# Layer 0's recurrence projections of a two-layer decoder trunk: three 256-column matmuls per weight block, or a 512- and a 256-column matmul and a fold

## The chip, the core and the metric

The kernel runs on one core of one Trainium2 chip. The metric is the device time of one execution in microseconds (us). The kernel before took 2241.95 us as the median of 3 runs (2240.21 to 2243.34).

The core has five engines with a queue each. PE (TensorE) multiplies a moving tile by a stationary block of 128x128 weights and adds the result up in a bank of PSUM, the memory behind it; the profile shows the load of the stationary block as PEld. DVE (VectorE) and ACT (ScalarE) do elementwise work and are the ones that read PSUM here. POOL and SP issue transfers. Every engine runs its instructions in the order in which the program was built, and waits at an instruction whose operands are not ready.

## The reference, cut to what matters

A sequence of 256 tokens of width 2048 goes through two layers and a final norm. Layer 0 mixes tokens by two recurrences:

```python
proj = h @ w_in                                   # 2048 x 6144
x_lru, y_lru, q_h, f_h, v_h, g_h = split(proj)    # six groups of 1024 columns
lru = rg_lru(causal_depthwise_conv(x_lru), ...)   # two gates, then a scan over tokens
lru = lru * gelu(y_lru)
hg = hgrn2(q_h, f_h, v_h, g_h, ...)               # 8 heads of 128, chunkwise
mix = concatenate([lru, hg]) @ w_out
```

Layer 1 is an attention layer; both layers end in a squared-ReLU MLP of width 8192. All data are float32, and the kernel keeps nearly that precision: each operand is split into a high part (rounded to the type that PE takes) and a low part (the rest), and a product is high x high + high x low + low x high.

## The kernel before, in words

**Units of weights.** Weights come in units of 128x2048 floats (1 MB), in a fixed list, by transfers that SP issues. `Weights.split` (L94 to L98) turns each half of a unit into `hi` (an ACT copy, L97) and `lo` (a DVE subtraction, L98). Three raw units, five `hi` halves and five `lo` halves are held at a time.

**A projection** (`project`, L305) multiplies one unit, 16 blocks of 128x128, by the 16 blocks of the activations `bufa`. Each activation block is 128x512: 256 columns of high part, then 256 columns of low part (one column a token). The result is one 128-column slice of the projection for all 256 tokens, added up in one bank `p` of PSUM; the pool `pmm` has three banks. Two ways of doing it stand in the kernel:

- `cross` (L163): for each block, the high weights against all 512 columns, which puts high x high in the bank's first half and high x low in the second; then, in a second pass over the 16 blocks, the low weights against the 256 high columns, into the second half as well. The two halves must be added when the bank is read. The MLP's first matrix and layer 1's q and k use it.
- `direct` (L169): for each block three matmuls of 256 columns, all into the first half. Nothing is left to add.

**Reading a bank in layer 0.** `scaled` (L360) writes the projection times the norm's factor `rs` to SBUF. For `direct` it is one DVE operation (L363). Otherwise ACT copies the second half to `t1` (L366), DVE adds the first half (L367) and DVE multiplies by `rs` (L368). Both ways stand under `urgent`, which the build's list scheduler ranks highest.

**The stage around the change** is layer 0's recurrence. Its steps stand in the list ORDER: `v0 h0 x0 h1 x1 h2 x2 h3 x3 v1 h4 x4 ... h7 x7 g0 y0 y1 y2 y3 g1 y4 y5 y6 y7`.

- `h` (`hgrn`, 8 heads): three projections (q, f, g), and between them a chain of levels: PE makes a 128x64 product `pl` twice (L423), DVE or ACT puts it in the score tile `st` (L426, L431, L433, L419), DVE multiplies `qk` by decay factors (L440), and the next level needs that. After eight levels come `po` (L447 to L449), a norm over a head (L453 to L458, with a chain of tiny DVE operations, L273 to L278), two transposes `pt` (L461), a multiplication by the gate (L467) and the split of the result into its block of `bufb` (L189 on ACT, L190 on DVE).
- `x` (`lru_in`, 8): one projection and a convolution (L477, L479).
- `g` (`lru_gates`, 2): eight small products of two blocks, which always use `direct`, then sigmoid, tanh, exp and sqrt on ACT (L158), each kind with a table load, and on DVE L497 to L506 with a scan over tokens.
- `y` (`lru_out`, 8): one projection, GeLU (ACT L513 and L158, DVE L514 to L517), and the split into `bufb`.
- `v` (2) makes values with `tokens` (512-column matmuls); it is not touched.

After the stage `w_out` follows: for each 512 columns of output, four units over the blocks of `bufb`, heads 0 to 3 first, then heads 4 to 7, then the two LRU groups.

`mm` (L145) chains all these matmuls in program order, so PE can't do a later projection first; the other products (`pl`, `po`, `pt`) are fitted in between by the scheduler, which lists instructions by an estimate of when each can run.

Of the kernel before, what the change touches and what calls it, by code (L numbers as in the profile page):

```python
# [40 lines left out]
def trunk_kernel(ctx, tc, x, xtok, cols, tab, masks, pos, fin, w_in, w_gate, w_out, w_qkv, w_o, w1, w2, out):  # L41
# [132 lines left out]
            mm(p, h, mov[:, S:], start=False, stop=False)  # L174
            mm(p, l, mov[:, :S], start=False, stop=last)

    HA, XA, YA = direct, direct, direct

    def folded(p, name="z", bufs=None):
        with urgent():  # L180
# [635 lines left out]
```

## Time and profile before

| | |
|---|---|
| time of the profiled execution | 2240.74 us |
| its span | 2239.0 us |
| granted TensorE clock over the span | 0.998 |
| layer 0's recurrence, about 21 to 336 us of the span | 32 projections and the first gates up to 280 us, then y0 to y3, the second gates and y4 to y7 |
| waits of PE from 21 to 431 us | 1.3 us at L447, 1.6 us for `bufa` and `lo` |

The profiled execution's time is 1.7 us more than its span. Times on the page are of this one execution. A row of a timeline or of a group gives an instruction's recorded duration; instructions of one engine overlap at their ends, so a queue's pace is read from the distance between starts. Idle time of an engine is put down to what ended it.

### The profile page before, as it was taken

Reading aid. Unit: us, or ns where it says so; the run is one execution under the profiler, and the core shown is the slowest. Engines: PE = TensorE matmul, PEld = TensorE weight load, DVE = VectorE, ACT = ScalarE, POOL = GpSimd, SP = SyncE. Lnnn points to the kernel's source line nnn. Section 1 sums busy time; section 2 is a strip of 40 time slices with the busy share of each in tenths; the row PEclk is TensorE's granted clock in tenths of the full one; section 3 lists DMA queues with packets and bytes.
Section 4 is the critical chain, followed back from the end, with each engine's and each line's share of the span. In section 5 each row is a group of like instructions: output and inputs, shape, how many; then the busy total and the mean of one; then the engine's idle time right before and its main releaser. Section 6 shows DMA issues by size and latency. Waiting matters only on the chain.

```text
span 2239.0 us, 30359 instructions
## 1 busy us (share of the span) xinstructions
PE 2218.6 (99%) x12196; PEld 1934.2 (86%) x12196; DVE 1409.1 (63%) x2212; ACT 1073.6 (48%) x1537; POOL 1.9 (0%) x7
## 2 busy tenths in 40 slices
PE   9999999999999999999999999999999999999997
PEld 8999998888888888888888888888888888888886
DVE  7777886565565565465567878556655645655654
ACT  6444585554444344344454445455434434434443
POOL 0000000000000000000000000000000000000000
PEclk9999999999999999999999999999999999999999
DMA  8444445455555555555554454555555555555553
GB/s 308 151 155 166 151 156 202 172 190 192 198 188 188 190 193 189 199 188 188 188 188 170 169 172 170 196 180 186 188 189 197 191 194 188 188 189 200 190 192 113
DMA packets 58717, 414.51 MB, mean 185 GB/s; under 512 B 6528, under 2 KB 7296, under 8 KB 9168
## 3 DMA queue, kind: packets, MB, share of 16 engines
q1 hardware_dynamic: 58320, 412.20, 52.4%
q8 instruction: 95, 1.56, 0.3%
q0 software_dynamic: 256, 0.38, 0.1%
q14 instruction: 46, 0.38, 0.1%
HBM read 410.70 MB, written 2.10 MB: 184 GB/s over the span
## 4 chain that ended last, share of the span: by engine, by line
PE 97%; ACT 1%; DVE 0%; issue 0%; DMA 0%; SPq 0%; ACTq 0%; DVEq 0%
PE p L146 94%; PE pl L423 1%; PE pl L548 0%; ACT hi L97 0%; PE pl L646 0%; DMA xall<-in_x 0%; PE po L667 0%; PE pd L659 0%; ACT L158 0%; DVE bufa L193 0%; PE pd L407 0%; PE pl L645 0%; ACT gi L158 0%; ACT bufa L192 0%; PE po L668 0%
## 5 line engine op out<-in xcount | busy, mean ns | idle before, releaser
L98 DVE TENSOR_TENSOR lo<-raw,hi 128x1024 fp32r<-128x1024 f32 (+1 forms) x774 | 932.1, 1220 | 603.1 <-ACT hi L97 431.8
L97 ACT CAST hi<-raw 128x1024 fp32r<-128x1024 f32 (+1 forms) x774 | 811.1, 1049 | 879.8 <-PE p L146 808.7
L146 PE MATMUL p<-bufa,hi 128*128 128x512 f32 (+1 forms) x3840 | 858.8, 357 | 3.1 <-DVE bufa L193 3.1
L146 PE MATMUL p<-hi,bufb 128*128 128x512 f32 x2560 | 793.9, 390 | 0.0
L146 PEld LDWEIGHTS p<-bufa,hi 128*128 128x128 f32 x3840 | 671.8, 189 | 95.4 <-DVE bufa L193 4.2
L146 PEld LDWEIGHTS p<-hi,bufb 128*128 128x128 f32 x2560 | 480.0, 188 | 98.7
L146 PE MATMUL p<-bufa,lo 128*128 128x256 f32 x3200 | 519.8, 284 | 0.0
L146 PE MATMUL p<-lo,bufb 128*128 128x512 f32 x1280 | 498.4, 389 | 0.0
L146 PEld LDWEIGHTS p<-bufa,lo 128*128 128x128 f32 x3200 | 451.5, 191 | 12.1
L146 PEld LDWEIGHTS p<-lo,bufb 128*128 128x128 f32 x1280 | 240.4, 188 | 49.4
L190 DVE TENSOR_TENSOR bufb<-z,bufb 128x256 fp32r<-128x256 f32 x136 | 57.7, 424 | 127.7 <-ACT bufb L189 127.7
L146 PE MATMUL p<-hi,bufa 128*128 128x512 f32 x384 | 122.6, 396 | 1.1 <-ACT hi L97 1.1
L182 ACT COPY t<-p 128x256 f32<-128x256 f32 x128 | 47.6, 372 | 111.7 <-PE p L146 111.7
L146 PEld LDWEIGHTS p<-hi,bufa 128*128 128x128 f32 x384 | 72.0, 188 | 16.5 <-ACT hi L97 2.0
L146 PE MATMUL p<-lo,bufa 128*128 128x512 f32 x192 | 76.3, 397 | 1.8 <-DVE lo L98 1.8
L189 ACT CAST bufb<-z 128x256 fp32r<-128x256 f32 x136 | 54.5, 401 | 17.2 <-DVE z L571 14.4
L536 DVE SCALAR_TENSOR_TENSOR xall<-p,nm,xall 128x512 f32<-128x512 f32 x64 | 47.8, 748 | 20.1 <-PE p L146 20.1
L571 DVE SCALAR_TENSOR_TENSOR z<-z 128x256 f32<-128x256 f32 x128 | 54.4, 425 | 4.4
L184 DVE TENSOR_TENSOR z<-p,t 128x256 f32<-128x256 f32 x128 | 53.3, 417 | 0.0
L247 ACT ACTIVATE z<-xall 128x512 bf16<-128x512 f32 x32 | 20.2, 631 | 54.5 <-DVE xall L536 54.5
L146 PEld LDWEIGHTS p<-lo,bufa 128*128 128x128 f32 x192 | 36.1, 188 | 10.5 <-DVE lo L98 3.7
L423 PE MATMUL pl<-qk 128*128 128x64 f32 x224 | 31.1, 261 | 0.0
(197 smaller groups left out, 729.1 us busy)
## 6 DMA issues: line engine op xcount, KB each, us to landing
raw<-in_w SPq DMA_DIRECT2D x256, 1024.0 KB, 4.8
raw<-in_w_qkv SPq DMA_DIRECT2D x48, 1024.0 KB, 4.8
raw<-in_w_in SPq DMA_DIRECT2D x46, 1024.0 KB, 4.8
raw<-in_w_out SPq DMA_DIRECT2D x16, 1024.0 KB, 4.8
raw<-in_w_o SPq DMA_DIRECT2D x16, 1024.0 KB, 4.8
xall<-in_xtok SPq DMA_DIRECT2D x1, 2048.0 KB, 9.3
raw<-in_w_gate SPq DMA_DIRECT2D x2, 1024.0 KB, 4.8
out<-xall SPq DMA_DIRECT2D x4, 512.0 KB, 4.0
```

The costliest lines, as they stand in the source:

```text
L97: A.copy(h, w)
L98: V.tensor_tensor(l, w, h.bitcast(F32), OP.subtract)
L146: chain[:] = [after(T.matmul(*args, **kw), chain)]
L182: A.copy(t, p[:, S:])
L184: V.tensor_tensor(z, p[:, :S], t, OP.add)
L189: A.copy(dst[:, :S], src)
L190: V.tensor_tensor(dst[:, S:], src, dst[:, :S].bitcast(F32), OP.subtract)
L247: A.activation(q, xres[:, j, n * 512:n * 512 + 512], AF.Square, accum_out=self.ss[:, j, n:n + 1])
L423: T.matmul(pl[:, j], kq[:, js], halves(qp[:, js], c, True), start=True, stop=True)
L536: V.scalar_tensor_tensor(xres[:, j, at], ps[j], 1.0 if scale is None else scale[:, j:j + 1], xres[:, j, at], op0=OP.mult, op1=OP.add)
L571: V.scalar_tensor_tensor(z, z, 0.0, z, op0=OP.max, op1=OP.mult)
```

## The change

The three names that choose how layer 0's projections are done go from `direct` to `cross`: `HA` (the 24 projections of the heads), `XA` (8, `lru_in`) and `YA` (8, `lru_out`).

```diff
-    HA, XA, YA = direct, direct, direct
+    HA, XA, YA = cross, cross, cross
```

Each of these 40 projections has 16 blocks, so 640 x 3 matmuls of 256 columns become 640 of 512 columns and 640 of 256, and the loads of stationary blocks go from 1920 to 1280. Through `scaled`, which asks `if acc is direct`, each bank is now read by L366 on ACT and by L367 and L368 on DVE in place of L363 on DVE. The gates keep `direct`. The units, the transfers and the list ORDER stay as they are; SP's and POOL's instructions keep their order. PE's, DVE's and ACT's order is made anew by the scheduler.

## The prediction

> **What bounds the kernel now.** I read the shares of busy time first, then the chain that ended last, then the timeline of PE in two stages, and last DVE's load by stretch and the waits.
>
> From the page, engine shares and the chain:
>
> ```profile
> PE 2218.6 (99%) x12196; PEld 1934.2 (86%) x12196; DVE 1409.1 (63%) x2212; ACT 1073.6 (48%) x1537; POOL 1.9 (0%) x7
> ...
> PE 97%; ACT 1%; DVE 0%; issue 0%; DMA 0%; SPq 0%; ACTq 0%; DVEq 0%
> ```
>
> PE sets the end nearly everywhere, so a change of PE's pace counts in full wherever DVE and ACT keep up. What matters is the pace (distance of starts), not the duration. PE's timeline, first in the recurrence (direct: hi, hi, lo), then in the MLP, where cross already runs:
>
> ```profile
> 281.11 0.40 PE L146 MATMUL p<-bufa,hi 128*128 128x256 f32 x2
> 281.35 0.28 PE L146 MATMUL p<-bufa,lo 128*128 128x256 f32 x1
> 281.47 0.40 PE L146 MATMUL p<-bufa,hi 128*128 128x256 f32 x2
> ```
>
> ```profile
> 501.06 3.82 PE L146 MATMUL p<-bufa,hi 128*128 128x512 f32 x16
> 504.71 2.08 PE L146 MATMUL p<-bufa,lo 128*128 128x256 f32 x16
> 506.63 3.82 PE L146 MATMUL p<-bufa,hi 128*128 128x512 f32 x16
> ```
>
> A block of direct takes 0.36 us (281.11 to 281.47; 0.1198 us a matmul over longer stretches), a projection 16 x 3 x 0.1198 = 5.75 us. Under cross, 16 matmuls of 512 columns take 3.65 us (0.228 each) and 16 of 256 take 1.92 us (0.120): 5.57 us.
>
> DVE's load decides the rest. Busy time by stretch, columns PE, PEld, DVE, ACT:
>
> ```profile
> 190.00:200.00 10.00, 10.00 (x87) 10.00 (x86) 8.30 (x17) 4.27 (x6) 0.00 (x0) 1.00 0.57 202
> ...
> 280.00:290.00 10.00, 10.00 (x86) 10.00 (x85) 7.21 (x14) 9.94 (x17) 0.00 (x0) 1.00 0.44 129
> 290.00:300.00 10.00, 8.71 (x74) 8.50 (x73) 9.34 (x20) 7.88 (x16) 0.00 (x0) 1.00 0.48 185
> 300.00:310.00 10.00, 10.00 (x86) 10.00 (x85) 10.00 (x30) 6.93 (x17) 0.52 (x1) 1.00 0.54 190
> ```
>
> Up to 270 us DVE is 69 to 89% busy. From the first gates (PE starts them at 273.17) to 340 us DVE or ACT is full. PE's one wait there is 1.3 us:
>
> ```profile
> 295.04 0.49 PE L447 MATMUL po<-vg,st 128*128 128x128 f32 x2 [1.29 <-ACT st L433]
> ```
>
> **The change, part by part.**
>
> *Matmuls.* 40 projections x (5.75 - 5.57) = **-7.2 us**, all on PE's path. The Trainium skill, "TensorE: Matmul & The Clock Gate", section "Back-to-back issue gap", has a matmul of N columns at N / 2.4 GHz + 2.5 ns: one saved fixed cost of 2.5 ns a block, an estimate of 1.6 us for 640 blocks, by which the sum below would be 5.6 us higher. The trace does not agree (0.228 against 2 x 0.1198, 11.5 ns a block), and the measurement decides.
>
> *The fold.* In place of L363 (0.335 us from start to start) come L366 on ACT (0.31) and L367 and L368 on DVE (0.335 each): 40 x 0.335 = 13.4 us more on DVE, 12.4 on ACT. Before the first gates DVE's idle share hides this: adding up DVE's queue of the changed order with the paces of the trace gives 37.0 us of work beside 47.4 of PE from h0's f to the second f, and 40.5 beside 49.8 in the last heads. A bank is released later by the copy's 0.3 us and DVE's queue; with three banks there are two projections, 11.1 us, of slack. Cost here: 0 if hidden; each us that DVE is late past that is 1 us. I take 1 us, near the 0 that the busy first half of DVE shows today; the upper end is 8 us, one us a head (the L447 wait of 1.3 us once a head).
>
> *What moves.* Because the folds rank as urgent, the scheduler lets the heads' level chains slide behind. In the order before, head 7 is at its third level when the first gates begin, and its transposes stand inside y5. In the changed order head 6 begins its first level there, and head 7's transposes stand in the second unit of w_out, two matmuls ahead of the block that needs their result. So ten levels and one and a half heads' norms come into the stretch in which DVE is full already. SP's and POOL's queues are as before, and nothing waits for a transfer.
>
> *That stretch, worked out.* Time 0 is PE's start of the first gates; paces as read from the trace (weight split on DVE 1.14, 256-column DVE operation 0.335, scan 0.60, predicated copy or tiny operation 0.20, ACT `hi` copy 0.94, ACT 256-column function 0.36, square root or copy 0.31, table load 1.28).
>
> 1. PE to the end of y1: 8 gate products x 0.72 + 2 x 5.57 + 5 level pairs x 0.366 + 6 small products x 0.12 = 19.5.
> 2. ACT then, in its new order: copy of y1, one sigmoid, 4 tanh, table, exp, `hi`, 3 exp, table, 2 sqrt, 2 small copies, third sqrt = 0.31 + 0.36 + 1.44 + 1.28 + 0.36 + 0.94 + 1.08 + 1.28 + 0.62 + 0.40 + 0.31 = 8.4. DVE's L504 waits for that sqrt: 27.9.
> 3. DVE from there to L467 of head 7: 15 weight splits 17.1, 8 scans 4.8, 70 operations of 256 columns 23.5, 40 short ones of 0.20 (5 level copies, 20 tiny norm steps, 4 of L500, 11 for the rotary tables, which are queued ahead too) 8.0, 4 of 0.12 0.5: 53.9. The same adding-up for the order before, from the first L497 to the last y's L517, gives 61.6 and with the 7.5 us of DVE idle that the waits show 69.1, beside some 70 on the trace; so I add 1.8%: 54.8. L467 starts at 82.7.
> 4. L467, ACT's split and DVE's split, 0.42 + 0.40 + 0.42: PE goes on at **84.0**.
>
> PE's own work to that matmul: 16 gate products 11.5, 8 projections 44.6, 35 w_out matmuls x 0.228 = 8.0, 14 level pairs 5.1, 18 small ones 2.2 = 71.4. PE is late by **12.6 us**: by my reading some 4 at the second gates (y2 and y3 still hold two of three banks), some 2 at w_out's second bank, the rest ahead of head 7's block. The 1.3 us at L447 goes: that wait's st copy is done by 31.0 and PE gets there at 31.2.
>
> Bounds: if ACT never delays DVE, L467 is bound by DVE's sum alone, 0.8 + 75.2 = 76.0 and PE at 77.2, 5.9 late; with as much DVE idle again as before's whole stretch (7.5), it is 16 to 20.
>
> *Sum.* -7.2 - 1.3 + 12.6 + 1 = **+5 us** on the profiled execution's 2240.74 (span 2239.0 and 1.7 around it), 2246; the median of the runs shown is 1.2 above that execution, so I forecast **2247 us**.
>
> **Rivals.**
>
> *A, the folds stay hidden (ends on the other side).* If DVE's real idle time in the tail is used up by the new order, so that L467 of head 7 starts within 4 us of PE's arrival, the sum is -7.2 - 1.3 + 1 + 0 to 4: 2234.5 to 2238. For: PE was never held by DVE's sum before, and the MLP runs cross at full pace. Against: DVE at 10.00 of 10 in 300 to 310, and step 3. It decides below a delay of 4 us. Chance 0.17; between it and the forecast (delay 4 to 8 us, 2238 to 2242) 0.1.
>
> *B, DVE late in the heads too.* Every level is a round of PE, DVE and PE, and a fold that sits ahead of L440 holds PE at the next L423. At 1 us a head, 8 us on top: 2250 to 2259. For: the slid levels show that DVE's time was short in the planned order; against: 81% load by step 2's sums. Chance 0.18.
>
> *C, the clock falls during the stall.* After the last matmul (2226.9) the granted clock is 1.00 to 2230, 0.80 in the next us and then 0.50, so it falls after 3.9 us without matmuls. Head 7's wait may be one gap of 6 us. Nothing in the trace shows the way back; between nothing and as long as the fall took at half pace it costs 0 to 2 us: 2247 to 2249. Inside the forecast; chance 0.3 of it. The Trainium skill, same page, section "What's actually happening", has the way back after a busy window of about 3.4 us, an estimate of 1.7 us.
>
> **How the numbers follow.** Forecast with C 0.55 (2242 to 2250, by the delay's bounds of 8 to 16), A 0.17, between 0.1, B 0.18. Leaving out half of A and a quarter of B gives the range 2236 to 2257. A measurement of this kernel tells about 0.2%, 4.5 us, from no change. Below 2237.5: 0.16; above 2246.4: B and the upper 6 in 10 of the forecast, 0.51; between: 0.33.
>
> **What would show it.** Right: 128x512 and 128x256 matmuls of the recurrence at 0.228 and 0.120 from start to start; no PE waits to speak of before the first gates; then some 12 us of PE idle from the first gates to w_out's second unit, put down to DVE or ACT, the longest ahead of head 7's block, right behind L461; DVE near 10 of 10 there. Wrong: the same pace but no such idle (A), or idle at L423 throughout (B), or matmuls of 512 columns slower than 0.228 beside DVE's and ACT's reads.

## The result, and the profile after

The changed kernel takes 2249.16 us (median of 7 executions, 2248.22 to 2251.92) against 2241.78 us for the kernel before (7 executions, 2240.21 to 2243.34). The ratio is 1.0034, with a 95% interval of 1.0024 to 1.0044: slower by 7.4 us. The forecast was 2247. The profiled execution took 2251.92 us (span 2250.2), 2.8 more than the median, and it is compared below with the profiled execution before, 2240.74 us: 11.2 us more.

Engine shares and the chain, from the page of the changed kernel:

```profile
PE 2220.6 (99%) x11556; PEld 1906.6 (85%) x11556; DVE 1417.7 (63%) x2252; ACT 1089.4 (48%) x1577; POOL 1.9 (0%) x7
...
PE 97%; DVE 1%; ACT 1%; DMA 0%; issue 0%; SPq 0%; ACTq 0%; DVEq 0%; POOLq 0%
```

PE has 640 instructions fewer, which by the pace alone should have taken some 7 us off, and is still busy 2.0 us longer, so some of its work became slower. DVE has 40 operations more, ACT 40. The chain's shares say little of this: DVE has gone from 0% to 1%.

PE's timeline in the heads (start, duration, line, names, moving tile, count):

```profile
226.51 2.07 PE L146 MATMUL p<-bufa,lo 128*128 128x256 f32 x16
228.42 0.86 PE L146 MATMUL p<-bufa,hi 128*128 128x512 f32 x3
...
236.21 3.82 PE L146 MATMUL p<-bufa,hi 128*128 128x512 f32 x16
239.87 0.28 PE L146 MATMUL p<-bufa,lo 128*128 128x256 f32 x1
```

Start to start, 16 matmuls of 256 columns take 1.91 us (0.119 each) and 16 of 512 take 3.66 (0.229): the new projections run at the pace of the MLP's.

The milestones show where the time went. The first gates' first matmul, in the kernel before and then in the changed one:

```profile
273.17 0.40 PE L146 MATMUL p<-bufb,hi 128*128 128x256 f32 x2
261.30 0.40 PE L146 MATMUL p<-bufb,hi 128*128 128x256 f32 x2
```

It starts **11.9 us earlier**: 32 x 0.18 = 5.8 are pace, and most of the rest is head work that now stands behind it (9 of 56 level pairs at 0.366 are 3.3, the ends of two heads, L418, L447 to L449 and L461, 1.1). The first MLP matmul starts at 435.43 in place of 425.76, **9.7 us later**. So the stretch between the two has grown by 21.5 us. PE's waits from 21 to 440 us, by what ended them (total, times, longest):

```profile
PE pt L461 <- ACT ho L458: 5.7, 1, 5.7
PE p L146 <- DVE z L367: 1.7, 1, 1.7
PE p L146 <- ACT gr L158: 1.3, 2, 0.7
PE po L447 <- ACT st L433: 1.1, 1, 1.1
PE p L146 <- ACT bufb L189: 1.0, 1, 1.0
PE po L448 <- ACT st L419: 0.7, 1, 0.7
```

With 0.2 at L423 they are 11.5 us from the first gates on (the rows are rounded), against 1.3 before, and none of them stands ahead of those gates. The longest is the one at head 7's transposes. DVE's timeline (the times in brackets are idle time and what ended it) shows what is late:

```profile
341.49 0.28 DVE L600 CAST ang<-ppi 32x256 f32<-32x256 int32 x1 [0.94 <-DMA ppi<-in_pos]
...
348.69 0.14 DVE L278 SCALAR_TENSOR_TENSOR hr<-rs,hr 128x2 f32<-128x2 f32 x1
...
350.06 0.42 DVE L467 TENSOR_TENSOR g<-pt,g 128x256 f32<-128x256 f32 x1
```

ACT's L458, and behind it PE's transposes at 349.29, wait for the last of head 7's tiny norm steps (L278). Between the first of these steps (L454 at 339.05) and the last stand weight splits, y operations, rotary-table operations (L600 to L610), and a wait for the positions' transfer, which the prediction had denied.

Busy time by stretch (first column the stretch's length, then PE, PEld, DVE, ACT, POOL, the granted clock, DMA share, GB/s):

```profile
190.00:200.00 10.00, 10.00 (x59) 8.74 (x58) 7.51 (x14) 5.05 (x10) 0.00 (x0) 1.00 0.57 188
...
300.00:310.00 10.00, 9.40 (x51) 9.02 (x52) 7.75 (x26) 4.58 (x11) 0.00 (x0) 0.66 0.31 105
330.00:340.00 10.00, 8.32 (x48) 7.19 (x47) 9.97 (x22) 5.55 (x16) 0.52 (x1) 1.00 0.59 191
340.00:350.00 10.00, 4.35 (x19) 3.03 (x17) 9.03 (x32) 4.68 (x9) 0.00 (x0) 0.91 0.37 127
```

In the heads (190 to 200) DVE has gone from 8.30 to 7.51 of 10 in spite of the folds, which fits level chains that have slid behind. From 340 to 350 PE works 4.35 of 10 beside a DVE at 9.03. And in 300 to 310 the clock column reads 0.66: PE is busy there, at half pace for most of it. Cut at the right places, the clock is either 1.00 or 0.50:

```profile
297.03:300.44 3.41, 2.09 (x14) 1.70 (x14) 3.41 (x8) 2.49 (x10) 0.00 (x0) 1.00 0.11 14
300.44:303.85 3.41, 2.85 (x14) 2.55 (x14) 3.41 (x10) 0.47 (x1) 0.00 (x0) 0.50 0.82 298
303.85:307.26 3.41, 3.41 (x18) 3.41 (x18) 1.61 (x8) 1.55 (x4) 0.00 (x0) 0.50 0.00 0
...
344.81:348.23 3.42, 0.00 (x0) 0.00 (x0) 3.42 (x14) 0.82 (x2) 0.00 (x0) 1.00 0.68 273
```

Taken as half of PE's busy time there, the loss is (2.85 + 3.41) / 2 = 3.1 us here, (1.40 + 3.41) / 2 = 2.4 in the two windows behind 348.23, and 1.7 in one at 1536.05, 7.2 us in all. That is a little too much, as PE's timeline in the last of the windows behind 348.23 shows:

```profile
351.99 1.05 PE L146 MATMUL p<-hi,bufb 128*128 128x512 f32 x2
352.84 0.63 PE L146 MATMUL p<-lo,bufb 128*128 128x512 f32 x1
353.27 1.05 PE L146 MATMUL p<-hi,bufb 128*128 128x512 f32 x2
```

From start to start a matmul of 512 columns takes 0.427 us here in place of 0.228, and from 301.36 on one of 256 columns takes 0.213 in place of 0.120, so 44 to 47% of the busy time is lost, some 6.6 us. The kernel before has no such window ahead of its last matmul. A wait in these rows begins only where the matmul before it ends, which is 0.16 us after the next could have started (0.28 long, 0.12 from start to start); for the seven more waits that is an estimate of 1.1 us. So the profiled difference is -7.2 (pace) + 10.2 (waits) + 1.1 (their edges) + 6.6 (half clock) = 10.7 of the 11.2 us; 0.5 is not assigned. For the median no trace tells how much half clock it holds. The profiled execution is the longest of the seven: the other six are 2.4 to 3.7 us shorter and show a granted clock of 0.996 over the span against its 0.995, so by that they held less of it.

### The profile page after: what moved, and what is told of

Same layout as the page of the kernel before. It is cut to its first block, busy times and chain, and to the rows that moved or that the text cites. A ratio compares the mean times of both kernels' runs of the same rounds, so it can differ in the third digit from the quotient of the medians.

```text
span 2250.2 us, 29113 instructions
## 1 busy us (share of the span) xinstructions
PE 2220.6 (99%) x11556; PEld 1906.6 (85%) x11556; DVE 1417.7 (63%) x2252; ACT 1089.4 (48%) x1577; POOL 1.9 (0%) x7
## 4 chain that ended last, share of the span: by engine, by line
PE 97%; DVE 1%; ACT 1%; DMA 0%; issue 0%; SPq 0%; ACTq 0%; DVEq 0%; POOLq 0%
PE p L146 94%; PE pl L423 1%; PE pl L548 0%; PE pl L646 0%; PE po L667 0%; DMA xall<-in_x 0%; PE pd L659 0%; DVE lo L98 0%; ACT hi L97 0%; DVE bufa L193 0%; DMA ppi<-in_pos 0%; ACT L158 0%; PE pd L407 0%; PE pl L645 0%; ACT bufa L192 0%
## 5 line engine op out<-in xcount | busy, mean ns | idle before, releaser
L146 PE MATMUL p<-bufa,hi 128*128 128x512 f32 x3200 | 779.1, 393 | 3.1 <-DVE bufa L193 3.1
L146 PEld LDWEIGHTS p<-bufa,hi 128*128 128x128 f32 x3200 | 587.0, 188 | 116.9 <-DVE bufa L193 4.2
L146 PE MATMUL p<-bufa,lo 128*128 128x256 f32 x3200 | 428.0, 284 | 0.0
L146 PEld LDWEIGHTS p<-bufa,lo 128*128 128x128 f32 x3200 | 413.6, 191 | 15.0
L182 ACT COPY t<-p 128x256 f32<-128x256 f32 x128 | 47.7, 372 | 112.9 <-PE p L146 112.9
L189 ACT CAST bufb<-z 128x256 fp32r<-128x256 f32 x136 | 54.6, 402 | 18.9 <-DVE z L571 14.4
L366 ACT COPY t<-p 128x256 f32<-128x256 f32 x72 | 26.8, 372 | 43.0 <-PE p L146 42.5
```

The source lines that it names most:

```text
L146: chain[:] = [after(T.matmul(*args, **kw), chain)]
L182: A.copy(t, p[:, S:])
L189: A.copy(dst[:, :S], src)
L366: A.copy(t, p[:, S:])
```

## The experiments

**Theory T**: the pace is gained, and lost again because head 7's chain arrives late in the queue of a DVE that is full behind the first gates, with a fall of the clock behind the waits. Rivals: the fold's work itself costs its price wherever it lies (F), the rotary tables and their transfer are the main cause (R), the clock falls for reasons of its own (D, L).

The results but those of two runs, which stand in their own sections (the kernel before took 2241.6 to 2241.8 us beside them; "waits" are PE's from 262 to 375 us of the profiled execution, "half clock" is half of PE's busy time at half clock from 262 to 1560 us of that execution, a little more than was lost):

| kernel | median us | ratio to before, 95% | waits us | half clock us |
|---|---|---|---|---|
| before | 2241.78 | | 1.3 | 0 |
| the change | 2249.16 | 1.0034 [1.0024, 1.0044] | 11.5 | 7.2 |
| no fold | 2244.81 | 1.0015 [1.0006, 1.0024] | 7.0 | 2.6 |
| direct with the fold's load | 2244.46 | 1.0015 [1.0006, 1.0024] | 3.2 | 1.7 |
| rotary tables later | 2247.50 | 1.0030 [1.0019, 1.0042] | 9.3 | 4.2 |
| w_out's order 2, 0, 1, 3 | 2245.58 | 1.0018 [1.0009, 1.0026] | 7.2 | 5.1 |
| both edits | 2240.22 | 0.9996 [0.9987, 1.0004] | 4.9 | 1.7 |
| both edits, y direct | 2240.92 | 0.9997 [0.9988, 1.0006] | 3.6 | 0 |
| before with both edits | 2242.84 | 1.0007 [0.9998, 1.0016] | 1.3 | 3.4 |
| heads direct | 2245.52 | 1.0019 [1.0010, 1.0028] | 4.8 | 4.9 |
| heads alone | 2242.32 | 1.0007 [0.9998, 1.0016] | 3.5 | 3.1 |
| both edits, y scale on GpSimd | 2240.73 | 1.0001 [0.9992, 1.0009] | 4.4 | 4.8 |

**No fold.** In `scaled`:

```diff
-            if acc is direct:
+            if acc in (direct, cross):
```

> The 40 projections keep the 512- and 256-column matmuls, but only the first half of the bank is read: no copy on ACT and no addition on DVE (this leaves out the terms high x low and low x high). The order of PE is nearly that of the change: head 7's transposes stand in w_out. Theory T (the loss is head 7's chain arriving late on DVE's queue behind the first gates, with the clock falling after the waits): 8 to 9 folds less on DVE behind the first gates are 2.9 us, so PE's waits between the first gates and w_out's second unit fall from 12.3 us to about 8, and the time is 2240 to 2245 us. Rival F (the fold's own work on DVE and ACT is the whole loss, wherever it lies): only the pace of PE is left, 2241.8 - 7.2 = 2234.6, at most 2236 us.

Measured 2244.81: in T's range, far from F's 2234.6. The new matmuls alone, with no fold anywhere, are slower than the kernel before. Head 7's wait, from the waits of PE:

```profile
PE pt L461 <- ACT ho L458: 4.1, 1, 4.1
```

Without folds DVE is earlier (the transposes start at 341.77 us, in the change at 349.29), but PE is there 4.1 us before it. So the faster PE and the slid order are enough for a loss of 3.2 us; the folds add 4.4 to it, the rest of the change's loss. And the order slides without any fold: 43 of 56 level pairs stand ahead of the first gates here, 42 in the change, 51 before.

**The fold's load on the matmuls of before.** With `direct` in all 40:

```diff
-                V.tensor_tensor(z, p[:, :S], rs, OP.mult)
+                t = tmp.tile([P, S], F32, name="t1", bufs=2)
+                A.copy(t, p[:, :S])
+                V.tensor_tensor(z, p[:, :S], t, OP.max)
+                V.tensor_tensor(z, z, rs, OP.mult)
```

> The three 256-column matmuls of the kernel before, with the fold's load put on top: a copy on ACT and one more 256-column operation on DVE for each of the 40 projections. PE's work is that of the kernel before. Theory T: the load alone brings DVE behind the first gates late by 2 to 3 us, less what PE's longer matmuls cover there: 2242 to 2246 us, PE's waits 3 to 7 us. Rival F (the load costs its price wherever it lies): as the change gained 7.2 on PE and lost 7.4 in all, the load costs 14.6 us: about 2256 us.

Measured 2244.46: T's range again, 11.5 us below F's. The waits are one of 2.0 us at w_out's second bank (for DVE's L365, the fold's place in this kernel) and 1.2 at the second gates, with one window of half clock behind the first. The load of 40 folds costs 2.8 us, and the waits it adds all stand behind the first gates. The folds alone hardly move the order: 50 of 56 level pairs stand ahead of the first gates.

**The rotary tables later.** `late0` is an anchor behind the first MLP's mean (a multiplication of r2 by one):

```diff
-    after(V.tensor_copy(ang, ppi), spot)
+    after(V.tensor_copy(ang, ppi), late0)
```

> The change, with the rotary tables (L600 and what follows on DVE) made to come after the first MLP's mean instead of in the queue ahead of head 7's last product. That takes 11 operations (3.1 us) and DVE's wait for the positions' transfer (0.9 us) out of the queue ahead of L467. Theory T with the rotary tables as one part of the queue: head 7's block 4 us earlier, PE's waits from 12.3 to 8 or 9 us, the time 2242 to 2246 us. Rival R (the transfer and the tables, which the prediction counted as waiting for nothing, are the main cause): waits below 5 us and 2238 to 2241 us. Rival N (that part of the queue isn't what ends last): within 1 us of the change, 2248 to 2250.

Measured 2247.50: between T (2242 to 2246) and N (2248 to 2250), and a miss for both. Head 7's wait fell from 5.65 to 3.4 us, by 2.2 where its block was expected 4 us earlier. The two windows of half clock at 300.44 aren't in this run's profiled execution, so the two profiled executions differ by more than the tables. The tables are a part of what is late, not the main one; R is out.

**w_out takes heads 4 to 7 last.** In the list of units, and alike where w_out is called:

```diff
-    units.extend((w_out, 4 * n + g) for n in range(4) for g in (2, 3, 0, 1))
+    units.extend((w_out, 4 * n + g) for n in range(4) for g in (2, 0, 1, 3))
```

> The change, with the first MLP-side product w_out taking its four row groups in the order 2, 0, 1, 3 in place of 2, 3, 0, 1, so that head 7's block comes in the fourth unit: some 11 us of PE work more ahead of it (the transposes stand 24 matmuls, 5.5 us, later). DVE's and ACT's work is unchanged. Theory T (lateness of one block): the 5.7 us wait at head 7's transposes goes, and the second fall of the clock with it (2 to 3 us): 2239 to 2243 us. Rival F (DVE's work is too much in that stretch, whatever PE does first): the wait moves to the next block, y7's or a later one, and the time stays within 2 us of the change, 2247 to 2250 us.

Measured 2245.58: 3.6 us gained, between the two ranges (T 2239 to 2243, F 2247 to 2250). PE's timeline:

```profile
348.71 0.73 PE L461 MATMUL pt<-tab__187,ho 128*128 128x128 f32 x2 [2.25 <-ACT ho L458]
```

The transposes stand 24 matmuls (5.5 us) later and still wait 2.25: DVE's timeline has two more weight splits ahead of head 7's last L278 than in the change (2 x 1.14 = 2.3 us), which in the change come behind it. So part of F's mechanism is real: the queue fills up with what comes next.

**Both edits.**

> The change with both edits: w_out's row groups in the order 2, 0, 1, 3, and the rotary tables behind the first MLP's mean. Theory T (head 7's chain is late by what is queued ahead of it on DVE, and a fall of the clock follows a long wait): the 2.3 us wait left at head 7's transposes with the order alone goes (the rotary edit alone took 2.3 us from it), and the 1.7 us that the half clock behind it cost with it; the waits of some 5 us at the second gates and at w_out's second bank stay: 2240 to 2243 us. Rival F (DVE's work fills up again): other work takes the rotary tables' place in the queue, as two weight splits did with the order alone, and the wait stays at 2 us or more: 2244.5 to 2247. Rival D (the falls of the clock come whatever PE waits for): wait gone but the half clock there all the same, 2243 to 2244.5.

Measured 2240.22, as T said. No wait is left at the transposes, and no half clock ahead of 1524 us: D is out. What remains, in the waits of PE:

```profile
PE p L146 <- DVE z L367: 1.7, 1, 1.7
PE p L146 <- ACT gr L158: 1.3, 2, 0.7
PE po L447 <- ACT st L433: 1.1, 1, 1.1
```

The change with these two edits is 8.9 us faster than without, and not to be told from the kernel before (0.9987 to 1.0004).

**Both edits on the kernel before**, as a control:

> The kernel before (three 256-column matmuls in all 40) with the same two edits: w_out's order 2, 0, 1, 3, and the rotary tables later. A control: the kernel before has one wait of 1.3 us in that stretch. Theory T: the edits have nothing more to free, 2240.5 to 2242.5 us. If the edits are worth something whatever the matmuls are, 2239 or less.

Measured 2242.84, 0.3 above the range. The edits are worth nothing there: they free only what the change had made late.

**Both edits, and the y projections direct** (`HA, XA, YA = cross, cross, direct`):

> As the run before it, but the eight y projections keep the three 256-column matmuls, so that no fold is left behind the first gates; heads and x projections (32 of 40) have the 512- and 256-column ones. PE's gain is 32 x 0.18 = 5.8 us. Theory T: with eight folds (2.7 us on DVE, 2.5 on ACT) less behind the first gates the wait at w_out's second bank goes and the one at the second gates is no longer than 1.3 us; what is left of waits is 2 to 4 us: 2237 to 2240.5 us, below the kernel before. Rival F: the heads' own folds ahead of the first gates have already made their chains late, and the waits are 5 us or more: 2241 us or above.

Measured 2240.92, just above T's range and short of 2241. The wait at w_out's second bank has gone, the waits are 3.6 us, and the profiled execution, without half clock, took 2238.88; nine of the other ten were 1.4 to 2.8 us longer. No version is shown to beat the kernel before.

**The heads direct, x and y with the new matmuls** (`HA, XA, YA = direct, cross, cross`):

> The change for the 16 x and y projections alone; the 24 head projections keep the three 256-column matmuls and have no fold. PE's gain is 16 x 0.18 = 2.9 us; eight folds lie behind the first gates. Theory T: heads' chains are not pushed behind the first gates (in the order of PE 50 of 56 level pairs stand ahead of them, 51 in the kernel before, 42 in the change), so PE's waits behind the first gates are 2 to 4 us: 2239.5 to 2243. Rival Y (the y projections' folds in the busy stretch are what costs, not the heads' late chains): waits 8 us or more, 2245 to 2249 us.

Measured 2245.52: T's range is missed, Y's time is met, though with waits of 4.8 us in place of 8. Here head 7 has been done since 330.89 (its L467), and PE's wait stands elsewhere:

```profile
339.63 0.77 PE L146 MATMUL p<-hi,bufb 128*128 128x512 f32 x1 [4.00 <-DVE z L367]
```

w_out's second bank waits for the last y's fold, behind weight splits on DVE (2.34 us for two at 335.73) and short operations. So T in its narrow form, head 7's chain alone, falls: what is late is whatever stands last in DVE's queue behind the gates, here a bank and there a head. One window of half clock (1.5 us) lies at that wait; the two others of this execution, at 434.81 and 1530.49, follow the waits for `bufa` that every kernel has.

**The heads alone** (`HA, XA, YA = cross, direct, direct`):

> The complement of the run with the heads direct: the 24 head projections alone have the 512- and 256-column matmuls and folds, the 16 x and y projections keep three 256-column ones. PE's gain is 24 x 0.18 = 4.3 us. 46 of 56 level pairs stand ahead of the first gates (51 in the kernel before, 42 in the change), head 7's transposes in w_out. Theory T (both parts load one queue on DVE, and a wait with its half clock costs only once DVE is late): with no y folds behind the gates head 7's wait is 1 to 4 us, with a half clock of 1.7 us behind it in most runs: 2240 to 2243.5 us, less than the sum of parts asks for. Rival S (each part costs its own share whatever the other does): the change's 7.4 less the 3.8 of the x and y part is 3.6: 2245.4, at least 2244.5 us.

Measured 2242.32, T's range. The wait is at head 7's block (2.8 us for ACT's L189) behind 0.5 at the transposes. The two parts alone lose 3.8 and 0.5 us and together 7.4: 3.1 more than their sum. S is out. One queue is loaded by both, and what one adds is late by all that the other has added. The waits say the same without the half clock: the parts add 3.5 and 2.2 us of them, both together 10.2.

**y0 and y1 ahead of the first gates.**

```diff
-ORDER = "... h7 x7 g0 y0 y1 y2 y3 g1 y4 y5 y6 y7"
+ORDER = "... h7 x7 y0 y1 g0 y2 y3 g1 y4 y5 y6 y7"
```

> The change with both edits (w_out's order 2, 0, 1, 3 and the rotary tables later), and the projections y0 and y1 placed ahead of the first gates in place of behind them. Theory T: the waits left at L447, L448 and the gates (3 us) come of head 6 and 7's chains having no PE work beside them there; 11 us of y projections ahead cover them: 2240.2 - 3 = 2237, 2235.5 to 2239 us. Rival G (what stands behind the gates on ACT and DVE decides): the gates' chain has 11 us less of PE work up to w_out, and the wait at w_out's second bank grows from 1.7 to 4 us or more with a half clock behind it: 2241 to 2246 us.

This kernel changes what is computed: y0 and y1 take `xc` before the scan has written it, and overwrite blocks of `bufb` that the gates read. It took 2249.41 us (ratio 1.0034, 1.0021 to 1.0046), far from T's range and above G's too. Its largest wait is 4.6 us at the second gates, for the gates' ACT work; w_out's second bank doesn't wait. As the first gates now hang on y1, it tells nothing of an order that could be used, and the waits at L447, L448 and the gates stay without an experiment of their own.

**The y projections' scale on GpSimd** (L368 of `lru_out` on the POOL engine):

> The change with both edits (w_out's order 2, 0, 1, 3 and the rotary tables later), and the multiplication by the norm (L368) of the eight y projections on GpSimd in place of DVE: 8 x 0.34 = 2.7 us less in DVE's queue behind the first gates. Theory T (DVE's queue is what is late): the 1.7 us wait for DVE's fold at w_out's second bank goes, 2237 to 2239.5 us against 2240.2 without it. Rival P (GpSimd's operation is so much longer than DVE's 0.34, or slows DVE beside it, that the y chains come later still): 2240.5 to 2244 us.

Measured 2240.73 against 2240.22 without it: P's range, if barely. The wait for DVE's fold went, and two of 0.6 us for the last block's split came. The operation takes 0.73 to 1.72 us on GpSimd (median 0.94; 0.42 on DVE), so the y chain may pay what DVE is spared; the two medians can't be told apart.

**Waits made on purpose, to see the clock.** On the kernel before, behind projection m = 8 of each MLP quarter, where PE else never waits:

```diff
+                if m == 8:
+                    gap(z, GAPS[4 * layer + q])
```

```python
def gap(z, n):      # GAPS = (0, 2, 1, 5, 3, 0, 10, 7)
    with urgent():
        for _ in range(n):
            V.tensor_scalar(z, z, 1.0, None, op0=OP.mult)
        late = psc.tile([P, 512], F32, name="pt", bufs=1)
        mm(late[:, :P], z[:, :P], ident, start=True, stop=True)
```

> The kernel before, with eight waits put into the MLPs, where PE otherwise never waits: behind the projection m = 8 of each quarter of each layer a 128x128 matmul (its result is not used) reads that projection's z after 0, 2, 1, 5, 3, 0, 10 and 7 more DVE operations of 0.34 us on z (each multiplies by one). By the paces of the trace (copy 0.31, two DVE operations of 0.34 and the ways between the engines) the waits should be some 1.2, 1.9, 1.5, 2.9, 2.2, 1.2, 4.6 and 3.6 us, 19 in all. Theory K (a wait itself brings the clock down, always from 2.0 us on, sometimes from 1.0, each time for 3.4 us or a multiple, 1.7 us of PE's work each): half clock behind the four waits of 2.2 us and more, now and then behind the shorter ones; 2241.8 + 19 + 4 to 7 times 1.7 = 2267.5 to 2273 us. Rival L (the falls belong to the crowded stretch behind the gates, whatever PE waits for): no half clock in the MLPs beyond the one at 1535 us, 2261 us.

Measured 2279.80 us (ratio 1.0175, 1.0161 to 1.0189), above both ranges. The waits were 1.83, 2.49, 2.16, 3.47, 2.82, 1.83, 5.11 and 4.13 us, 23.8 where 19 was expected, as DVE was still at weight splits when the projection ended. Half clock, as half of the busy time, is 15.1 us of the profiled execution's two MLPs, all but 1.7 of it (at 431) behind the made waits, in a stage without gates or crowding: L is out. K is right in kind and wrong in its rule: half clock came behind one wait of 1.83 us (at 482) and not behind one of 2.16 (at 843) or the other of 1.83 (at 1774). Cut into windows of 3.413 us:

```profile
479.43:482.84 3.41, 1.58 (x12) 1.29 (x11) 2.83 (x4) 0.37 (x1) 0.00 (x0) 1.00 0.36 86
482.84:486.26 3.42, 3.42 (x10) 2.68 (x9) 0.53 (x2) 1.14 (x2) 0.00 (x0) 0.50 0.52 220
486.26:489.67 3.41, 3.41 (x24) 3.15 (x23) 0.87 (x1) 1.36 (x2) 0.00 (x0) 1.00 0.00 0
...
841.24:844.65 3.41, 1.61 (x8) 1.39 (x9) 2.32 (x5) 0.51 (x2) 0.00 (x0) 1.00 0.65 235
844.65:848.07 3.42, 3.42 (x21) 2.97 (x20) 0.24 (x1) 1.83 (x2) 0.00 (x0) 1.00 0.17 72
1773.07:1776.48 3.41, 2.04 (x10) 1.74 (x11) 2.17 (x4) 0.41 (x2) 0.00 (x0) 1.00 0.77 233
```

Every fall and rise of this execution lies on one grid: 482.84 + 53 x 3.413 = 663.7, + 158 x 3.413 = 1022.1, + 326 x 3.413 = 1595.5, within 0.1 us of the next falls. What counts, as far as these rows show it, is how much of a grid window PE was idle. Idle 1.83 of 3.41 us in the window ahead of 482.84 brings the next window to half; the 1.83 us at 1774 are split by the grid into 0.45 and 1.37 and bring nothing.

## Why the prediction was right

- *Matmuls, -7.2 us.* Right: 0.229 and 0.119 from start to start. Of the 11.9 us by which the first gates are earlier, pace (5.8) and moved work (4.4) make 10.2; 1.7 isn't assigned.
- *The fold ahead of the gates, 1 us.* It cost nothing: no wait of PE stands there. Rival B falls with it.
- *What moves.* The new order was read rightly, and it is the center of it: the stretch behind the gates is 21.5 us longer, of which 10.2 are added waits, some 5 half clock and 4.4 the slid work itself. The reason given, that the folds rank as urgent, was wrong: without folds the chains slide all the same (43 of 56 level pairs ahead of the gates), and folds on the old matmuls leave 50 there. It is the new matmuls that move the scheduler's order; by which of its estimates stays open. The sentence "nothing waits for a transfer" was wrong too. POOL issues the positions' transfer (ppi) only when PE has done head 7's L449, which slid too: at 337.53 us (300.5 before), landing 3.9 later, so that DVE waits 0.9 us at L600. With the tables out of the queue head 7's wait was 2.2 us shorter.
- *The stretch, worked out.* The waits came out nearly as forecast, 11.5 us for 12.6, but two errors hide in that, and that they met is luck. L467 was forecast at 82.7 us behind PE's start of the gates and stood at 88.8; head 7's block at 84.0, it stood at 89.7. DVE's first L504 stands at 28.9 for 27.9, and from there to L467 DVE works 53.8 us, for a forecast 53.9; what was mis-sized is its idle time, 6.1 us where 0.9 was added. The longest of it is for the gates' square root on ACT:

```profile
321.54 0.43 DVE L504 SCALAR_TENSOR_TENSOR gi<-gr,gi 128x256 f32<-128x256 f32 x1 [2.08 <-ACT gi L158]
```

  So DVE was late, but not only by its own queue. PE was late on its side too: without the waits it took 78.1 us to that block, for 71.4; some 3 of the difference are half clock. The places of the waits: 2 us at w_out's second bank (1.7 measured), the rest ahead of head 7's block (6.6 for some 6.6, though 5.65 of it ahead of the transposes and not behind them), but 3.3 in place of 4 at L447, L448, L423 and the second gates, with 1.8 of that at L447 and L448: the 1.3 at L447 did not go, as was predicted, but became 1.1, with another 0.7 behind it.
- *Rival C, 0 to 2 us.* It came true and is **the term that was mis-sized most**: some 6.6 us in the profiled execution, the longest of its kernel. I took the clock to fall behind one gap of some 6 us, since the end of the trace before showed it falling some 4 us after the last matmul (3.7; the prediction has 3.9). It fell as well in the choppy stretch ahead of 300.44, where no wait exceeds 1.1 us, and at 1536.05. The Trainium skill, "TensorE: Matmul & The Clock Gate", section "What's actually happening", has the clock halved after at least one idle window of about 3.4 us, back after a busy one, in windows that run freely of the kernel. The free-running windows and the way back agree with these traces; the idle window does not: 1.32 us idle of 3.41 sufficed once (297.03 to 300.44).
- *Rival A, the folds stay hidden.* It did not come: the delay was 11.5 us, its point 4. Even with no folds the new matmuls lose 3.2 us, so to hide the folds would not have been enough.

The sum of +5 was worked out for the profiled execution, and there it became +11.2; between the medians it is +7.4. Waits were somewhat smaller than forecast, half clock larger, and the heads cost nothing. That the median came within 2.2 us of the forecast is luck in part: the profiled execution before is 1.0 us below its median, the one after 2.8 above. That the same terms make up the median's 7.4 in the proportion of the profiled execution is not shown.

## What to carry to other kernels

A faster bound engine is worth its gain only where the others have slack: here the gain ahead of the gates was given back in the next stage, where PE came 11.9 us earlier to a DVE that was already full. So look for the stage in which the second engine is at 10 of 10 and ask what slides into it, count the time in which that engine itself waits for others as well as its work, and whose transfer hangs on the slid work. Put the consumer of the latest chain last (here w_out's row group of heads 4 to 7) and take work that nobody needs yet (the rotary tables) out of the queue: that took back 8.9 us, while each edit alone took back 3.6 and 1.7.

## What the runs showed of the hardware

The half clock goes by a grid of 3.413 us windows, and each window is at 1.00 or 0.50 as a whole. In the traces of all fourteen kernels here, from 20 us to the last matmul, PE idle for 1.81 us or more of a window at full clock was always followed by half clock in the next, idle for 1.30 or less never, and in between it came at times: after 1.32 in the change and after 1.53 in the change and the heads-direct kernel, not after 1.53 in direct with the fold's load, 1.66 with both edits or 1.80 among the made waits. What decides there isn't settled. The way back is sharper: a window at half clock in which PE was busy for 2.87 us or less was followed by another at half clock, one with 3.02 or more by full clock.

A window at half clock costs a PE that is busy throughout 1.5 to 1.6 us, by the paces of 0.213 for 0.120 and 0.427 for 0.228. So the same 1.5 us of waits for `bufa` at about 1530 us, which every kernel has, cost 1.5 in one execution and 3.1 in another. The executions of the kernel before that ran beside the experiments fall into three groups, 2240.0 to 2240.5, 2241.5 to 2242.1 and 2243.0 to 2243.6 us, with none between; the granted clock over the span is 0.998 in all of the first and 0.997 in all of the third. Steps of 1.5 us fit no, one and two windows at half clock, behind the waits for `bufa` at 431 and 1524 us. That this is why executions of one kernel differ so is likely, but no two executions of one kernel were traced.
